# A decoder step on one core: the first half-step in the form of the second (one microbatch alone, two by seven products for eight), its down sums in PSUM, and the state-space matrices made in larger batches

## The chip, the cores and the metric

The kernel runs on one core of one Trainium2 chip, with one launch. The metric is device time in microseconds (us) of that core; the time before is the median of three runs. All data are fp32. TensorE (PE) multiplies, VectorE (DVE), ScalarE (ACT) and GpSimd (POOL) work on tiles, and DMA transfers are issued from two queues here: SyncE's (SP), which loads, and ACT's, which mostly stores. Each engine takes its instructions in the order of its own queue.

## The reference

One decoder layer, run on a prompt of 1024 tokens and 8 x 4 sample tokens that share the weights. With D = 1024 and D_FF = 2816 = 22 x 128:

```python
def swiglu(x, w_gate, w_up, w_down):
    return (silu(x @ w_gate) * (x @ w_up)) @ w_down

h = h + 0.5 * rms_norm(swiglu(rms_norm(h, g_pre), w_gate1, w_up1, w_down1), g_post)   # first half-step
z = rms_norm(h, g_mix) @ w_in                 # -> u (state-space input), q, k, v
# u: 32 groups of a complex diagonal state-space scan (state 64, width 16), gelu, gate
# q, k, v: sliding-window attention (window 128), rotary, sinks
h = h + rms_norm(concat(norm(y_ssm), norm(o)) @ w_out, g)
h = h + rms_norm(memory_attend(rms_norm(h, g), mem_k, mem_v), g)
h = h + 0.5 * rms_norm(swiglu(rms_norm(h, g_pre), w_gate2, w_up2, w_down2), g_post)   # second half-step
```

The change touches the two half-steps and the making of the state-space matrices (`s5_discretise` and the powers of the discretised state, which depend on weights alone).

## The kernel before

**Tokens and precision.** The 1056 tokens are three microbatches t = 0, 1, 2 of NT = 352 columns; t = 2 holds the last prompt tokens and the samples. Activations lie transposed, 8 chunks of 128 features by 352 tokens. A product of fp32 matrices is made of three matmuls (`PASSES`): weight and activation are each split into a rounded high part (an ACT copy) and the rest (a DVE subtraction). `loadw` does so for a weight: one transfer of 512 KB into one of two `raw` buffers, ACT (L99), DVE (L100), into one of six `w` tiles. One row block of weight (1024 wide) feeds 24 matmuls of 128x128 by 128x352 for each microbatch.

**First half-step (`ffn`, L393).** For each g of 11 (two of the 22 hidden blocks), gate and up are computed for all three microbatches with the same split weights (`gate_up`, L223: matmuls of L105), the hidden tiles `hid` stay in SBUF, and `down` (L235, matmuls of L241) follows for each microbatch; the part sums of each g leave PSUM through a DVE addition into an SBUF sum (L247). In the gaps between, `filler()` draws one step of `ssm_prep`, a generator: tables by powers of two for four groups at a time (`tables`), then matrices of one group at a time (`groups`), stored in DRAM scratch `sp`; the matrix M goes through a padded DRAM tile `kp`, written and read back on ACT's queue (L723, L725). `finish1` does the post-norm, the residual and the next pre-norm.

**Second half-step.** Microbatch 0 goes alone through `ffn_one` (L252), gate, up and down interleaved as above. Microbatches 1 and 2 then form a 2x2 block product with seven products for eight: `pair_operands` (L273) makes sums and differences of the two and splits them (L280) into `xq` slots of 4 x 352; `pair_weights` (L298) does the same for two weight row blocks, 512 wide; `pair_products` (L326) multiplies, matmuls of L330; `pair_gate_up` writes the hidden to DRAM `hs`. `pair_down` (L373, matmuls of L385) reads it back for each hidden block k, splits it, and sums all 22 blocks in PSUM. PSUM has eight banks, of which six (`bank`) and two (`pbank`) can be had. The first of the two downs uses all eight at once (parts `((0, 8),)`), the second goes through the blocks twice with four banks each (parts `((0, 4), (4, 4))`), so that each 512-wide piece of weight feeds 12 matmuls.

**Order.** The program is written with a priority for each piece and put into each engine's queue by a planner that simulates the engines. The order of a queue is then fixed; a wait in it holds up all behind it on that engine.

Of the kernel before, what the change touches and what calls it, by code (L numbers as in the profile page):

```python
# [6 lines left out]
F32 = mybir.dt.float32  # L7
# [15 lines left out]
PASSES = ((0, 0), (0, 1), (1, 0))  # L23
G_FFN1_PRE, G_FFN1_POST, G_MIX_PRE, G_MIX_POST, G_XA_PRE, G_XA_POST, G_FFN2_PRE, G_FFN2_POST, G_MEM, G_CAT = range(10)
# [3 lines left out]
def decoder_step(tc, a, o):  # L28
# [194 lines left out]
    def gate_up(x, w, h, j):  # L223
        pg, pu = bank(), bank()
        for p, ww in ((pg, w[0]), (pu, w[1])):
            for k in range(8):
                mm3(p[:, :NT], ww, k * 128, x, k, k == 0, k == 7)
        s, u = R("sg", [128, NT], 2), Q()
        v.tensor_mul(s, pg[:, :NT], x[2])  # L229
        sc.activation(s, s, AF.Silu)  # L230
        v.tensor_mul(u, pu[:, :NT], x[2])  # L231
        v.tensor_mul(s, s, u)  # L232
        split(s, h[:, j, 0], h[:, j, 1])

    def down(acc, w, h, first):  # L235
        for cs in (range(4), range(4, 8)):
            p = {c: bank() for c in cs}
            for j in range(2):
                for c in cs:
                    for i, (wa, xa) in enumerate(PASSES):  # L240
                        pe.matmul(p[c][:, :NT], w[j][:, wa, c * 128:c * 128 + 128], h[:, j, xa],  # L241
                                  start=j == 0 and i == 0, stop=j == 1 and i == 2)
            for c in cs:
                if first:
                    sc.activation(acc[:, c], p[c][:, :NT], AF.Copy)
                else:
                    v.tensor_add(acc[:, c], acc[:, c], p[c][:, :NT])  # L247

    def hidden(bufs):
        return R("hid", [128, 2, 2, NT], bufs, F32R)  # L250

    def ffn_one(x, wg, wu, wd, home):  # L252
        acc, held = None, None
        for g in range(NH // 2 + 1):
            now = None
            if g < NH // 2:
                ws = [(loadw(wg[2 * g + j]), loadw(wu[2 * g + j])) for j in range(2)]
                now = hidden(2)
                for j in range(2):
                    gate_up(x, ws[j], now, j)  # L260
            if held is not None:
                ds = [loadw(wd[2 * (g - 1) + j]) for j in range(2)]
                acc = K8(home) if acc is None else acc
                down(acc, ds, held, g == 1)
            held = now
        return acc
# [3 lines left out]
    def slot(dtype=F32R):  # L270
        return xp[0].tile([128, 4, NT], dtype, name="xq", tag="xq", bufs=12)

    def pair_operands(ya, yb, home):  # L273
# [8 lines left out]

        t3 = slot(F32)
# [69 lines left out]
    def pair_gate_up(x, wg, wu, hs, home):  # L353
# [7 lines left out]
        for j in range(NH // 2):  # L361
# [11 lines left out]
    def pair_down(wd, hs, i, y, parts):  # L373
        for c0, n in parts:
            p = [bank() if c < 6 else pbank() for c in range(n)]
            for k in range(NH):
                h, x = slot(), R("raw2", [128, 1024], 2)[:, :NT]
                hi, lo = h[:, 0], h[:, 1]
                sy.dma_start(x, hs[k][:, i])
                sc.activation(hi, x, AF.Copy)  # L380
                v.tensor_sub(lo, x, hi.bitcast(F32))
                w = loadw(wd[k][:, c0 * 128:(c0 + n) * 128], width=n * 128)
                for c in range(n):
                    for q, (wa, xa) in enumerate(PASSES):
                        pe.matmul(p[c][:, :NT], w[:, wa, c * 128:c * 128 + 128], (hi, lo)[xa],  # L385
                                  start=k == 0 and q == 0, stop=k == NH - 1 and q == 2)
            for c in range(n):
                if c % 2:
                    v.tensor_copy(y[:, c0 + c], p[c][:, :NT])
                else:  # L390
                    sc.activation(y[:, c0 + c], p[c][:, :NT], AF.Copy)

    def ffn(xn, wg, wu, wd, order, home, finish, filler, ready=None):  # L393
        acc = {}

        for g in range(NH // 2):
            if g == 0 and ready:
                ws, ds = ready
            else:
                ws = [(loadw(wg[2 * g + j]), loadw(wu[2 * g + j])) for j in range(2)]  # L400
                ds = [loadw(wd[2 * g + j]) for j in range(2)]
            hid = {}

            def gu(t):
                hid[t] = hidden(3)
                for j in range(2):
                    gate_up(xn[t], ws[j], hid[t], j)
                    filler()

            last = g == NH // 2 - 1  # L410
            for n in (0, 1, 3, 4, 2, 5) if last else (0, 1, 3, 2, 4, 5):
                what, t = "down" if n > 2 else "gu", order[n % 3]
                if what == "gu":
                    gu(t)
                else:
                    if g == 0:
                        acc[t] = K8(home[t])
                    down(acc[t], ds, hid[t], g == 0)
                    if last:
                        finish(t, acc[t])  # L420
                    else:
                        filler()
# [30 lines left out]
    rd = scratch("rd", [128, 256])  # L453
    hd = [[scratch(f"h{i}_{t}", [128, 8, NT]) for t in range(3)] for i in range(3)]
# [48 lines left out]
    def ssm_prep():  # L503
# [21 lines left out]
        par = take(97)  # L525
        ar, ai, ls, s1 = par[:, 0:32], par[:, 32:64], par[:, 64:96], par[:, 96:97]
# [118 lines left out]

        def tables(q):
            pos[0] = base
            C = take(512).rearrange("p (g c) -> p g c", c=128)
            Z = take(512).rearrange("p (g c) -> p g c", c=128)
            u = take(256).rearrange("p (g c) -> p g c", c=64)  # L650
            w = take(256).rearrange("p (g c) -> p g c", c=64)
            v.memset(C[:, :, 0], 1.0)
            v.memset(Z[:, :, 0], 0.0)
            for k in range(7):
                m = 1 << k
                bc = TBC[:, k, 4 * q:4 * q + 4][:, :, None].to_broadcast([128, 4, m])
                bs = TBS[:, k, 4 * q:4 * q + 4][:, :, None].to_broadcast([128, 4, m])
                tt(u[:, :, :m], C[:, :, :m], bc)
                tt(w[:, :, :m], Z[:, :, :m], bs)
                tt(C[:, :, m:2 * m], u[:, :, :m], w[:, :, :m], ALU.subtract)  # L660
                tt(u[:, :, :m], C[:, :, :m], bs)
                tt(w[:, :, :m], Z[:, :, :m], bc)
                tt(Z[:, :, m:2 * m], u[:, :, :m], w[:, :, :m], ALU.add)
            for i in range(4):
                sc.dma_start(spd[4 * q + i][:, SP_COS:SP_COS + 128], C[:, i])
                sc.dma_start(spd[4 * q + i][:, SP_SIN:SP_SIN + 128], Z[:, i])

        def groups(q):
# [17 lines left out]
            wt, out = take(128), take(528)  # L686
            w8, cx = out[:, 0:256], out[:, 256:528]
            clx, cls = cx[:, 0:144], cx[:, 144:272]
            t1, t2 = take(144), take(144)

            def j3(x, n=9):
                return x.rearrange("p (j h) -> p j h", h=16)[:, :n]

            for i in range(4):
                g = 4 * q + i

                def hb(x, n):
                    return x[:, i][:, None, :].to_broadcast([128, n, 16])

                def jb(x, j0, n):  # L700
                    return x[:, g, j0:j0 + n][:, :, None].to_broadcast([128, n, 16])

                tt(j3(t1), hb(C1, 9), jb(LR, 0, 9))
                tt(j3(t2), hb(C2, 9), jb(LI, 0, 9))
# [25 lines left out]
        for _ in range(11):  # L730
            yield
# [795 lines left out]
```

## Time and profile before

| what | value |
|---|---|
| median of 3 runs | 2355.25 us (2351.96 to 2357.52) |
| profiled execution | 2350.7 us, span 2348.9 us |
| granted TensorE clock, mean | 0.986 |
| first half-step and first projection | 0 to about 895 us of the span |
| state-space, attention, memory parts | about 895 to 1596 us |
| second half-step | about 1596 us to the end |
| moved by DMA | 272 MB, mean 116 GB/s |

The profile is of one execution; a term worked out from it stands against 2350.7 us, which is 4.55 us under the median. In rows of stretches the columns are: from:to, length, busy time of each engine with its number of instructions, granted clock, share of DMA time, GB/s. In rows of groups they are: line, engine, operation, output and input with their shapes, count, busy us, mean ns of one, and the idle time of the engine just before them with what ended it. In a timeline they are start, duration, engine and line; SPq and ACTq are the issuing of transfers from these queues.

### The profile page before, as it was taken

The page shows a single profiled execution, that of the slowest core. Times are in us where ns is not written, and L with a number is a line of the kernel's source. Part 1 is how long each engine was busy: PE and PEld are TensorE (multiplying, and loading weights), DVE is VectorE, ACT ScalarE, POOL GpSimd, SP SyncE. Part 2 cuts the span into 40 slices and gives each one's busy share as a digit, 9 for nine tenths or more (in the row PEclk, how much of TensorE's full clock was granted, in tenths as well). Part 3 has the DMA queues.
Part 4 walks back from the last instruction along what each step waited for, and adds up shares of the span by engine and source line. Part 5 has one row for each costly group of instructions (what it writes and reads, how often), then busy time and mean ns, then how long its engine had stood idle before and what let it go on. Part 6 is the DMA issues. An engine that isn't in the chain of part 4 may idle for free.

```text
span 2348.9 us, 37434 instructions
## 1 busy us (share of the span) xinstructions
PE 2281.9 (97%) x14425; PEld 2178.3 (93%) x14425; DVE 1631.5 (69%) x4004; ACT 839.4 (36%) x1645; POOL 15.9 (1%) x54
## 2 busy tenths in 40 slices
PE   8999999999999899999799989999999899999997
PEld 8999999999999899888699869999999899999996
DVE  8756556665664877777768855588866987776464
ACT  6322111211212433535545323354433434344443
POOL 0000000000000000000000000000000000000000
PEclk9999999999999999999899999999999999999998
DMA  4222212221213321544135562165544243326663
GB/s 171 70 71 68 62 57 71 82 76 59 73 55 93 112 87 58 193 147 127 35 97 167 183 221 72 55 213 169 175 132 144 85 143 106 115 97 200 185 193 119
DMA packets 112194, 272.39 MB, mean 116 GB/s; under 512 B 13168, under 2 KB 54128, under 8 KB 110576
## 3 DMA queue, kind: packets, MB, share of 16 engines
q1 hardware_dynamic: 78976, 227.81, 30.8%
q10 hardware_dynamic: 33040, 42.20, 5.1%
q8 instruction: 113, 1.85, 0.3%
q14 instruction: 65, 0.53, 0.1%
HBM read 229.87 MB, written 43.20 MB: 116 GB/s over the span
## 4 chain that ended last, share of the span: by engine, by line
PE 85%; DVE 7%; DMA 5%; ACT 2%; issue 1%; ACTq 0%; SPq 0%; DVEq 0%
PE mm L105 39%; PE mm L241 14%; PE mm L330 13%; PE mm L385 3%; PE px L105 3%; DMA raw<-wd 2%; DVE w L100 1%; PE cv L1279 1%; PE cs L1254 1%; PE px L1176 1%; DVE K L219 1%; PE ac L877 1%; PE px L495 1%; PE px L385 1%; DMA K<-h 1%
## 5 line engine op out<-in xcount | busy, mean ns | idle before, releaser
L105 PE MATMUL mm<-X,w 128*128 128x352 f32 x6384 | 1060.8, 325 | 12.3 <-ACT X L195 6.5
L105 PEld LDWEIGHTS mm<-X,w 128*128 128x128 f32 x6384 | 1028.3, 189 | 30.2 <-ACT X L195 8.5
L99 ACT ACTIVATE w<-raw 128x1024 fp32r<-128x1024 f32 (+1 forms) x271 | 266.2, 988 | 500.4 <-PE mm L105 212.2
L100 DVE TENSOR_TENSOR w<-raw,w 128x1024 fp32r<-128x1024 f32 (+1 forms) x271 | 307.1, 1136 | 136.2 <-ACT w L99 134.0
L241 PE MATMUL mm<-hid,w 128*128 128x352 f32 x2112 | 358.6, 328 | 12.6 <-DVE K L247 6.2
L241 PEld LDWEIGHTS mm<-hid,w 128*128 128x128 f32 x2112 | 345.6, 189 | 19.7 <-DVE K L247 8.8
L330 PE MATMUL mm<-xq,w 128*128 128x352 f32 x1584 | 263.5, 323 | 0.0
L330 PEld LDWEIGHTS mm<-xq,w 128*128 128x128 f32 x1584 | 255.9, 188 | 0.4 <-ACT w L310 0.4
L247 DVE TENSOR_TENSOR K<-K,mm 128x352 f32<-128x352 f32 x320 | 158.3, 518 | 52.2 <-PE mm L241 51.3
L514 DVE TENSOR_TENSOR K<-K 128x128 f32<-128x128 f32 (+7 forms) x796 | 171.6, 250 | 11.3 <-DMA sp<-K 2.0
L385 PE MATMUL mm<-xq,w 128*128 128x352 f32 x924 | 159.1, 326 | 4.6 <-ACT w L99 3.4
L385 PEld LDWEIGHTS mm<-xq,w 128*128 128x128 f32 x924 | 148.8, 188 | 10.7 <-ACT w L99 5.9
L310 ACT ACTIVATE w<-raw 128x512 fp32r<-128x512 f32 x154 | 90.0, 625 | 119.1 <-PE mm L330 83.1
L231 DVE TENSOR_TENSOR q<-mm,rs 128x352 f32<-128x352 f32 x88 | 46.0, 522 | 117.6 <-PE mm L105 117.6
L311 DVE TENSOR_TENSOR w<-raw,w 128x512 fp32r<-128x512 f32 x154 | 101.1, 686 | 6.2 <-ACT w L310 3.9
L116 DVE TENSOR_TENSOR tot<-tot,sq 128x352 f32<-128x352 f32 x179 | 93.0, 520 | 10.4 <-ACT sq L114 7.0
L114 ACT ACTIVATE sq<-K 128x352 f32<-128x352 f32 x170 | 81.9, 490 | 42.7 <-DVE tot L116 34.7
L229 DVE TENSOR_TENSOR sg<-mm,rs 128x352 f32<-128x352 f32 x88 | 46.0, 523 | 72.9 <-PE mm L105 72.5
L183 ACT ACTIVATE hid<-sg 128x352 fp32r<-128x352 f32 x88 | 43.6, 496 | 145.7 <-DVE sg L232 115.7
L230 ACT ACTIVATE sg<-sg 128x352 f32<-128x352 f32 x88 | 43.2, 492 | 138.9 <-DVE sg L229 120.4
L195 ACT ACTIVATE X<-K,c_gains 128x352 fp32r<-128x352 f32 x80 | 44.0, 580 | 45.4 <-DVE K L220 42.8
L184 DVE TENSOR_TENSOR hid<-sg,hid 128x352 fp32r<-128x352 f32 x88 | 45.8, 521 | 15.6 <-ACT hid L183 15.4
(326 smaller groups left out, 2179.1 us busy)
## 6 DMA issues: line engine op xcount, KB each, us to landing
raw<-wd SPq DMA_DIRECT2D x66, 512.0 KB
raw<-wu SPq DMA_DIRECT2D x65, 512.0 KB
raw<-wg SPq DMA_DIRECT2D x64, 512.0 KB
sp<-sp SPq DMA_DIRECT2D x16, 848.0 KB
h<-K ACTq DMA_DIRECT2D x9, 1408.0 KB
raw<-hs SPq DMA_DIRECT2D x66, 176.0 KB
raw<-wd SPq DMA_DIRECT2D x44, 256.0 KB
K<-xT SPq DMA_DIRECT2D x24, 352.0 KB
```

The costliest lines, as they stand in the source:

```text
L99: sc.activation(w[:, 0], raw, AF.Copy)
L100: v.tensor_sub(w[:, 1], raw, w[:, 0].bitcast(F32))
L105: pe.matmul(p, w[:, wa, col:col + 128], x[xa][:, k, :n], start=first and i == 0, stop=last and i == 2)
L114: sc.activation(q, c, AF.Square)
L116: eng.tensor_add(tot, tot, q)
L241: pe.matmul(p[c][:, :NT], w[j][:, wa, c * 128:c * 128 + 128], h[:, j, xa], start=j == 0 and i == 0, stop=j == 1 and i == 2)
L247: v.tensor_add(acc[:, c], acc[:, c], p[c][:, :NT])
L310: sc.activation(w[:, 0], x, AF.Copy)
L311: v.tensor_sub(w[:, 1], x, w[:, 0].bitcast(F32))
L330: pe.matmul(p, w[a_][:, wa, k * 128:k * 128 + 128], x[b_][xa][:, k], start=start and k == 0 and i == 0, stop=stop and k == 3 and i == 2, s ...
L385: pe.matmul(p[c][:, :NT], w[:, wa, c * 128:c * 128 + 128], (hi, lo)[xa], start=k == 0 and q == 0, stop=k == NH - 1 and q == 2)
L514: v.tensor_tensor(out, x, y, op)
```

## The change

Both half-steps get the same form. In the first, microbatch `ta` = 2 goes alone through gate and up for all 22 blocks, then its down; then `tb` = 0 and `tc_` = 1 go through gate and up as a pair by seven products, then their two downs. In the second, microbatch 0 alone also does all its gate and up first, then its down. The hidden goes to DRAM (`h1`, `h2`) and is read back for the down, in pairs of blocks (`hidden(2)`, two buffers) instead of `xq` slots; all down sums stay in PSUM over the 22 blocks. The parts are `((0, 8),)` for a microbatch alone, where the scale `rs` is applied as the sum is moved out, and `((0, 4), (4, 4))` for both of the pair in the first half-step. `xq` has 8 slots instead of 12. Between the pieces, `step` draws the preparation by a table: `F_A = (0, 0, 1, 1)` steps per piece.

```diff
+F_A = (0, 0, 1, 1)
-    def gate_up(x, w, h, j):
+    def gate_up(x, w, out):
...
-        v.tensor_mul(u, pu[:, :NT], x[2])
-        v.tensor_mul(s, s, u)
-        split(s, h[:, j, 0], h[:, j, 1])
+        v.tensor_mul(s, s, pu[:, :NT])
+        sc.dma_start(out, s)
-    def down(acc, w, h, first):
-        for cs in (range(4), range(4, 8)):
...
-                    v.tensor_add(acc[:, c], acc[:, c], p[c][:, :NT])
+    def down(wd, h, y, parts, rs=None, filler=lambda: None):
+        for c0, n in parts:
+            p = [bank() if c < 6 else pbank() for c in range(n)]
+            for k in range(NH):
+                if k % 2 == 0:
+                    pair = hidden(2)
+                x = R("raw2", [128, 1024], 2)[:, :NT]
+                hi, lo = pair[:, k % 2, 0], pair[:, k % 2, 1]
+                sy.dma_start(x, h[k])
+                sc.activation(hi, x, AF.Copy)
+                v.tensor_sub(lo, x, hi.bitcast(F32))
+                w = loadw(wd[k][:, c0 * 128:(c0 + n) * 128], width=n * 128)
+                for c in range(n):
+                    for q, (wa, xa) in enumerate(PASSES):
+                        pe.matmul(p[c][:, :NT], w[:, wa, c * 128:c * 128 + 128], (hi, lo)[xa],
+                                  start=k == 0 and q == 0, stop=k == NH - 1 and q == 2)
+                filler()
...
+    for j in range(NH):
+        ws = pre[2 * j:2 * j + 2] if j < 2 else (loadw(a["wg1"][j]), loadw(a["wu1"][j]))
+        gate_up(xa, ws, h1[j][:, 2])
+        if 5 <= j and j % 2:
+            step()
+        if j == 3:
+            for t in (tb, tc_):
+                xr[t] = load_x(t, a["xT"][t])
+                norm_in_place(xr[t], G_FFN1_PRE)
+    y = K8(ta)
+    down(a["wd1"], [h[:, 2] for h in h1], y, ((0, 8),), xa[2], lambda: step(F_A[1]))
+    ops = pair_operands(xr[tb], xr[tc_], tc_, ta)
+    post1(ta, y)
+    pair_gate_up(ops, a["wg1"], a["wu1"], [h[:, 0:2] for h in h1], tb, lambda: step(F_A[2]))
...
+    pre1(ta, y)
+    for i, t in enumerate((tb, tc_)):
+        y = K8((tc_, tb)[i])
+        down(a["wd1"], [h[:, i] for h in h1], y, ((0, 4), (4, 4)), filler=lambda: step(F_A[3]))
+        if i:
+            for _ in prep:
+                pass
+        marks[t] = tc.cur_priority
+        post1(t, y, load_x((ta, 3)[i], a["xT"][t]))
+        pre1(t, y)
...
+    for j in range(NH):
+        gate_up(xn[0], (loadw(a["wg2"][j]), loadw(a["wu2"][j])), h2[j][:, 2])
+    y = K8(3)
+    down(a["wd2"], [h[:, 2] for h in h2], y, ((0, 8),), xn[0][2])
```

In the preparation, one doubling works on cosine and sine together (`double`), the first 16 columns for all 32 groups at once, the rest for four groups; two groups at a time are made into matrices, with one transposition and one small product each, and M goes through a zeroed scratch `kd`:

```diff
+        def double(T, tmp, k, gs, n):
+            m = 1 << k
+            bc, bs = (t[:, k, gs][:, None, :, None].to_broadcast([128, 2, n, m]) for t in (TBC, TBS))
+            u = tmp[:, :2 * n * m].rearrange("p (z g m) -> p z g m", z=2, m=m)
+            tt(T[:, :, :, m:2 * m], T[:, :, :, :m], bc)
+            tt(u, T[:, :, :, :m], bs)
+            tt(T[:, 0, :, m:2 * m], T[:, 0, :, m:2 * m], u[:, 1], ALU.subtract)
+            tt(T[:, 1, :, m:2 * m], T[:, 1, :, m:2 * m], u[:, 0], ALU.add)
...
-            for i in range(4):
+            for i in (0, 2):
...
+                for n in range(2):
+                    pe.transpose(p3[:, n], wt[:, n], ident)
...
-                sc.dma_start(kd, kp[:16])
...
+                sc.dma_start(kd[g:g + 2, :, 128:256].rearrange("g h c -> h g c"),
+                             kp[:16].rearrange("h (g c) -> h g c", g=2))
```

Where it moves instructions, in the queues of the two programs. First PE in the first half-step, about the first weight blocks of before: a gate and up of one microbatch (L105), a down of two hidden blocks (96 matmuls of L241), the next gate and up.

```order
203 L105 MATMUL mm<-X_290,w 128x352
204 L105 MATMUL mm<-X_289,w 128x352 x2
205 L105 MATMUL mm<-X_290,w 128x352
206 L105 MATMUL mm<-X_289,w 128x352
207 L241 MATMUL mm<-hid,w 128x352 x96
208 L105 MATMUL mm<-X_134,w 128x352
209 L105 MATMUL mm<-X_135,w 128x352
```

After, at the end of the 22 gates and ups of microbatch 2 (L106), its whole down begins (L252); `mm` are six of its banks, `px` two.

```order
711 L106 MATMUL mm<-X_166,w 128x352
712 L106 MATMUL mm<-X_165,w 128x352
713 L252 MATMUL mm<-hid,w 128x352 x15
714 L252 MATMUL px<-hid,w 128x352 x6
715 L252 MATMUL mm<-hid,w 128x352 x21
716 L252 MATMUL px<-hid,w 128x352 x6
```

The downs, which lay between the gates and ups, have moved behind all of them, as 528 matmuls in a row.

Second, ACT in the first half-step, where it makes the matrices of one group before: weight splits (L99), the copies of the transposed product (L715, L716), of M (L721), a hidden split (L183), and the stores, with the write and the reading back of `kp` (L723, L725).

```order
360 L99 ACTIVATE w<-raw 128x1024
361 L715 ACTIVATE K_411<-px 128x128
362 L716 ACTIVATE K_411<-px 128x64
363 L721 ACTIVATE kp<-px 16x128
364 L183 ACTIVATE hid<-sg 128x352
365 L726 DMA sp_114<-K_411 128x192
366 L723 DMA kp_5883<-kp 16x256
367 L727 DMA sp_114<-K_411 128x272
368 L725 DMA sp_114<-kp_5883 128x1x128
369 L99 ACTIVATE w<-raw 128x1024 x2
```

After, in the first half-width down (`tb`, parts `((0, 4), (4, 4))`): hidden splits (L247) and 512-wide weight splits (L100), with the work of one pair of groups between.

```order
528 L247 ACTIVATE hid<-raw_6523 128x352
529 L100 ACTIVATE w<-raw 128x512 x2
530 L694 DMA sp_116<-K_707 256x1x192
531 L700 DMA kd<-kp 16x2x128
532 L684 DMA sp_117<-K_707 256x1x144
533 L705 DMA sp_116<-kd 128x1x128 x2
534 L682 ACTIVATE K_707<-K_707 64x2x128
535 L685 DMA sp_117<-K_707 128x1x128
536 L686 DMA sp_117<-K_707 128x1x128
537 L692 ACTIVATE K_707<-px 128x2x128
538 L693 ACTIVATE K_707<-px 128x2x64
539 L699 ACTIVATE kp<-px 16x256
```

A group's work has moved from between gates and ups of three microbatches into a loop of narrow weight splits, two groups at a time.

Third, DVE in the second half-step, where microbatch 0 ends and the pair begins. Before, the operands' sums (L284, L285) and splits (L280) lie among the last additions of the down (L247), the last gate's product and the pair's first weights (L311 and following).

```order
2434 L285 TENSOR_TENSOR K_15541<-K_15541,K_15148 128x1408
2435 L247 TENSOR_TENSOR K_16191<-K_16191,mm 128x352 x2
2436 L317 TENSOR_TENSOR raw<-raw 128x512
2437 L247 TENSOR_TENSOR K_16191<-K_16191,mm 128x352
2438 L280 TENSOR_TENSOR xq<-xq 128x1408
2439 L247 TENSOR_TENSOR K_16191<-K_16191,mm 128x352
2440 L184 TENSOR_TENSOR hid<-sg,hid 128x352
2441 L247 TENSOR_TENSOR K_16191<-K_16191,mm 128x352
2442 L280 TENSOR_TENSOR xq<-K_15148,xq 128x1408
```

After, they come right behind the last gate and up of microbatch 0 (L235), ahead of the down's third pair of hidden blocks (L248).

```order
2431 L235 TENSOR_TENSOR sg<-sg,mm 128x352
2432 L282 TENSOR_TENSOR xq<-K_15552 128x1408
2433 L101 TENSOR_TENSOR w<-raw,w 128x1024
2434 L283 TENSOR_TENSOR K_15552<-K_15552,K_15159 128x1408
2435 L275 TENSOR_TENSOR X_18210<-K_15159,X_18210 128x1408
2436 L275 TENSOR_TENSOR xq<-xq 128x1408
2437 L275 TENSOR_TENSOR xq<-K_15159,xq 128x1408
2438 L101 TENSOR_TENSOR w<-raw,w 128x1024
2439 L275 TENSOR_TENSOR xq<-K_15552,xq 128x1408
2440 L248 TENSOR_TENSOR hid<-raw_17492,hid 128x352
2441 L248 TENSOR_TENSOR hid<-raw_17525,hid 128x352
```

The operands have moved from the end of the down to its beginning. In all, the built programs have 13522 and 13248 matmuls on PE (the first half-step's gates, ups and downs 4752 and 4488), 3991 and 3608 instructions on DVE, 550 and 826 transfers in SP's queue, 257 and 284 in ACT's, 44 and 12 fills on POOL.

More of the change, by code (lines that the diff above doesn't have):

```diff
@@ L220, in postnorm, with hidden @@
             v.tensor_add(y[:, k], resid(k), y[:, k])
-    def gate_up(x, w, h, j):
+    def hidden(bufs):
+        return R("hid", [128, 2, 2, NT], bufs, F32R)
+    def gate_up(x, w, out):
         pg, pu = bank(), bank()
@@ L227, in gate_up @@
                 mm3(p[:, :NT], ww, k * 128, x, k, k == 0, k == 7)
-        s, u = R("sg", [128, NT], 2), Q()
+        s = R("sg", [128, NT], 2)
         v.tensor_mul(s, pg[:, :NT], x[2])
         sc.activation(s, s, AF.Silu)
-        v.tensor_mul(u, pu[:, :NT], x[2])
-        v.tensor_mul(s, s, u)
-        split(s, h[:, j, 0], h[:, j, 1])
-    def down(acc, w, h, first):
-        for cs in (range(4), range(4, 8)):
[L237 to L245, printed above, removed]
-                else:
-                    v.tensor_add(acc[:, c], acc[:, c], p[c][:, :NT])
@@ L249, in hidden @@
[L249 to L266, printed above, removed]
+        v.tensor_mul(s, s, pu[:, :NT])
@@ L281, in halves_of, with both @@
             ops[name] = (hi, lo)
+        def both(x):
+            return x[:, 0:4], x[:, 4:8]
         t3 = slot(F32)
@@ L371, in pair_gate_up @@
                 sc.dma_start(hs[2 * j + i], h[:, 2 * i:2 * i + 2])
[L373 to L422, printed above, removed]
+            filler()
@@ L425, in decoder_step, with norm_in_place, by_chunk, get @@
+    def norm_in_place(y, gi):
+        rs = rstd_wide(sqsum([y[:, k] for k in range(8)]))
+        for k in range(8):
+            v.scalar_tensor_tensor(y[:, k], y[:, k], gain(gi, k), rs, op0=ALU.mult, op1=ALU.mult)
+    def by_chunk(src):
+        def get(k):
+            x = total()
+            sy.dma_start(x, src[:, k])
+            return x
+        return get
     gains = cload(const, "gains", [128, 88])
@@ L649, in tables @@
[L649 to L663, printed above, removed]
+            T = take(1024).rearrange("p (z g c) -> p z g c", z=2, c=128)
@@ L685, in groups, with j4 @@
             tt(bb2, bb2, t64, ALU.add)
[L686 to L692, printed above, removed]
-            for i in range(4):
+            clx, t2, wt, w8 = (take(n).rearrange("p (g c) -> p g c", g=2) for n in (288, 288, 256, 384))
+            def j4(x, n):
+                return x.rearrange("p g (j h) -> p g j h", h=16)[:, :, :n]
@@ L1359, in after_o @@
             return
-        rs = rstd_wide(sqsum([y[:, k] for k in range(8)]), tag="rs", bufs=3)
-        for k in range(8):
-            v.scalar_tensor_tensor(y[:, k], y[:, k], gain(G_FFN2_PRE, k), rs, op0=ALU.mult, op1=ALU.mult)
+        norm_in_place(y, G_FFN2_PRE)
         xn[t] = y
```

161 lines of the change are left out of this document (89 added, 72 removed).

## The prediction

> **What bounds the kernel now.** I read the page first.
>
> ```profile
> span 2348.9 us, 37434 instructions
> PE 2281.9 (97%) x14425; PEld 2178.3 (93%) x14425; DVE 1631.5 (69%) x4004; ACT 839.4 (36%) x1645; POOL 15.9 (1%) x54
> PE 85%; DVE 7%; DMA 5%; ACT 2%; issue 1%; ACTq 0%; SPq 0%; DVEq 0%
> ```
>
> TensorE is busy for 97% and carries 85% of the chain that ended last, so only two things move the time: fewer matmuls, or fewer microseconds in which PE does less than it could. The next view is busy time in stretches (columns: stretch; its length, then PE, PEld, DVE, ACT, POOL busy and instructions; granted clock; DMA share; GB/s). 0 to 895.2 is the first half-step with the state-space preparation beside it and, at its end, the first projection; 1596 to 1870 is the second half-step's microbatch alone, 1880 to 2140 its pair by seven products, then two down stages.
>
> ```profile
> 0.00:50.00 50.00, 41.60 (x234) 39.83 (x235) 43.05 (x149) 34.58 (x67) 0.59 (x6) 0.97 0.55 200
> 50.00:750.00 700.00, 699.91 (x4328) 685.93 (x4327) 449.56 (x1375) 146.08 (x298) 5.84 (x30) 1.00 0.23 68
> 750.00:895.20 145.20, 136.80 (x830) 134.08 (x829) 100.28 (x249) 48.72 (x94) 1.96 (x2) 0.94 0.27 92
> 1820.00:1880.00 60.00, 52.57 (x309) 50.33 (x308) 56.54 (x95) 29.22 (x45) 0.00 (x0) 0.97 0.26 84
> 1880.00:2140.00 260.00, 260.00 (x1625) 260.00 (x1624) 200.56 (x342) 104.95 (x178) 0.00 (x0) 1.00 0.36 117
> 2140.00:2226.00 86.00, 86.00 (x536) 86.00 (x534) 43.03 (x57) 34.03 (x52) 0.00 (x0) 1.00 0.68 213
> 2270.00:2320.00 50.00, 45.98 (x263) 41.46 (x262) 24.61 (x43) 22.23 (x44) 0.00 (x0) 1.00 0.59 181
> ```
>
> The same view for single lines gives the yardstick: what one 128x352 matmul costs where nothing waits (L330, the seven products), and how many of them each stretch of the first half-step held (L105 gate, up and projection; L241 down), with the prep's own matmuls (L714, L720).
>
> ```profile
> 1900.00:2142.00 242.00, 242.00 (x1512) 242.00 (x1510) 1.00 0.35 115
> ...
> 0.00:50.00 50.00, 37.25 (x192) 34.37 (x192) 0.97 0.55 200
> 50.00:750.00 700.00, 453.75 (x2796) 447.60 (x2797) 1.00 0.23 68
> 750.00:895.20 145.20, 104.91 (x614) 100.08 (x613) 0.94 0.27 92
> ...
> 0.00:50.00 50.00, 1.88 (x12) 2.04 (x13) 0.97 0.55 200
> 50.00:750.00 700.00, 238.98 (x1430) 231.22 (x1428) 1.00 0.23 68
> 750.00:895.20 145.20, 27.53 (x144) 26.11 (x144) 0.94 0.27 92
> ...
> 50.00:750.00 700.00, 8.67 (x32) 4.55 (x32) 1.00 0.23 68
> ...
> 50.00:750.00 700.00, 12.56 (x64) 3.56 (x64) 1.00 0.23 68
> ```
>
> 242.00/1512 is 0.160 us per matmul. By it the first 50 us hold 204 x 0.160 = 33 us of work (17 lost), the next 700 hold 4226 x 0.160 = 676 (24 lost), the last 145.2 hold 758 x 0.160 = 121 (24 lost). The page's busy share hides this, because neighbouring matmuls overlap in it.
>
> **The change, part by part, against the profiled run (2350.7 us, 4.6 under the median of 2355.25).**
>
> *Seven products for eight in the first half-step.* Gate and up of two microbatches go from 2112 matmuls to 1848: 264 x 0.160 = **-42.2 us**. This is on the path, since PE bounds that stretch, and the built program has the 264 fewer.
>
> *Start.* What PE waits for in the first half-step:
>
> ```profile
> PE mm L105 <- ACT X L195: 6.5, 1, 6.5
> PE mm L241 <- ACT hid L183: 3.1, 1, 3.1
> PE mm L241 <- DVE hid L184: 2.8, 1, 2.8
> ```
>
> The 6.5 us until the first X is ready stay. Of the other 11 of the 17 lost I take **-4** (0 to -8): only one microbatch is prepared at first, the other two load at the fourth weight pair under PE work.
>
> *Down sums stay in PSUM.* Vanishing adds:
>
> ```profile
> L247 DVE TENSOR_TENSOR K<-K,mm 128x352 f32<-128x352 f32 x320 | 158.3, 518 | 52.2 <-PE mm L241 51.3
> ```
>
> They free DVE, which is no bound (450 of 700 us). For PE only the gaps at gate/down borders count: of the 24 us lost in 50 to 750, the prep's matmuls take between half of their busy 21.2 (busy spans overlap; a 0.160 matmul shows 0.325) and all of it. I take 15 for them, which stay, and **-9** (-3 to -13).
>
> *End of the first half-step.* Today all three microbatches finish together in the last 145 us: the waits of 3.1 and 2.8 above, and a clock of 0.94 (0.06 x 145 = 8.7 us). Now two are normed under later downs, and one is left at the end: 24 lost becomes about 9, **-15** (0 to -20).
>
> *Half-width downs, the price of the change.* With two accumulating downs in 4+4 banks, every 512-wide piece of weight carries 12 matmuls, 12 x 0.160 = 1.92 us. The kernel already does this once, in its last down (L385; its window, its weight splits on ACT, PE's and ACT's waits there):
>
> ```profile
> 2231.20:2328.00 96.80, 91.32 (x529) 84.14 (x527) 1.00 0.57 175
> ...
> L99 ACT ACTIVATE w<-raw x26: 629/632/637, 2267.5 to 2324.6; 128x512 fp32r<-128x512 f32 x26
> ...
> PE mm L385 <- ACT w L99: 3.4, 6, 1.6
> ...
> ACT w L99 <- DMA raw<-wd: 33.6, 23, 2.9
> ```
>
> 529 matmuls take 96.8 us where 84.6 would do; weights come one per (2324.6-2267.5)/25 = 2.28 us. The timeline shows why: two raw buffers, each reloaded only after both splits.
>
> ```profile
> 2266.01 0.33 SPq L92 DMA_DIRECT2D raw<-wd  x1
> ...
> 2269.31 0.63 ACT L99 ACTIVATE w<-raw 128x512 fp32r<-128x512 f32 x1 [0.81 <-DMA raw<-wd]
> ...
> 2269.97 0.69 DVE L100 TENSOR_TENSOR w<-raw,w 128x512 fp32r<-128x512 f32 x1 [0.70 <-ACT w L99]
> ...
> 2270.70 0.33 SPq L92 DMA_DIRECT2D raw<-wd  x1
> ```
>
> Issue to landing 3.3, ACT 0.63, DVE 0.69: 4.69 us for one buffer, two pieces per cycle, 2.35 each. The first half-step gets 2 downs x 2 halves x 22 = 88 such pieces: between 88 x 0.28 (12.2/44, the down as a whole) = 25 and 88 x (2.35 - 1.92) = 38. The hidden tiles come on the same SP queue there too, so the row fits. I take 26, less 6 for the six split weights PE has ahead at the start of the first: **+20** (0 if the loop keeps up, 38). SP's queue, 550 transfers before and 826 after, is no bound: four issues of 0.33 to 0.37 in a cycle of 4.69. The full-width down of one microbatch is free: 86.00 of 86.00 busy in 2140 to 2226.
>
> A rule of the Trainium skill speaks against this stage: "TensorE: Matmul & The Clock Gate", section "HAM oscillation", says that a loop over K with compute per tile shorter than its wait for data lets the clock drop to half at every tile, once the idle time passes about 3.4 us. The row of 2270 to 2320 shows 1.00 in just this loop, with waits of 0.6 us on average, so the sum goes by the row; by the rule it would be rival four.
>
> *Preparation in larger batches.* Prep's tensor operations leave DVE about 380 instructions shorter, off the path (POOL's memsets, 44 to 12, too: 15.9 us busy in all). What is on the path is where it now lies. Nothing but its tables runs in the first down, 22 steps run in the pair, and 7 group pairs in the first half-width down, where ACT feeds PE: four activations and seven DMA issues each on ACT's queue, two of them waiting for a write to return. Rows of before for the pieces:
>
> ```profile
> 224.36 0.39 ACTq L723 DMA_DIRECT2D kp<-kp  x1
> ...
> 225.88 0.66 ACTq L725 DMA_DIRECT2D sp<-kp  x1
> ...
> ACT w L99 <- DMA sp<-K: 14.2, 1, 14.2
> ```
>
> From that write's issue to the read's are 1.5 us; with five more issues of 0.33 to 0.39 and the activations (some 0.3 each) I estimate 4.7 us of ACT per pair of groups, beside a loop that already lacks time; part lies in ACT's idle share (50 - 22 of 50). I take **+10** for the seven (0 to 20). The 14.2 us row shows how long a weight split can stand behind a store.
>
> *Pair under prep.* DVE is 200.56/260 = 77% busy in the second half-step's pair, without a loss. Here prep's groups come on top:
>
> ```profile
> L514 DVE TENSOR_TENSOR K<-K 128x128 f32<-128x128 f32 (+7 forms) x796 | 171.6, 250 | 11.3 <-DMA sp<-K 2.0
> ```
>
> Halved in number, the group part is by estimate 57 of these (a third, at larger tiles); two thirds of it in the pair make 37 us, so 91%. Since DVE works in order, a late split then stalls PE: **+6** (0 to 15). Norms that stand ahead of weight splits in DVE's queue during half-width downs: 24 operations of 0.5 us for each microbatch, **+5** (0 to 10). First half-step: -42.2-4-9-15+20+10+6+5 = -29.
>
> *Second half-step.* The 303 matmuls between 1820 and 1880 need 48.5 us; 11.5 are lost where the operands are made after the last gate:
>
> ```profile
> PE mm L241 <- DVE K L247: 5.0, 5, 2.0
> PE mm L330 <- ACT w L310: 2.4, 1, 2.4
> L280 DVE TENSOR_TENSOR xq<-K,xq 128x1408 fp32r<-128x1408 f32 x5 | 8.0, 1615 | 0.0
> ```
>
> Now a whole down (528 x 0.160 = 84 us) lies between, under which the operands are made. In DVE's order seven operations of that size or nearly (L282, L283, four L275, with two weight splits of 1.2) come before the third hidden pair: about 12.5 us, which PE needs 15.5 us after the start of the down (four pieces x 24 x 0.160). Five weights are ready (19 us). **-11.5** and **+1** (0 to 5). The last two downs take the hidden in pairs, four pieces ahead instead of a dozen slots: **+2** (0 to 4). Together -8.5.
>
> Sum: -29.2 - 8.5 = **-37.7**: 2313 for the profiled run, 2355.25 - 37.7 = 2317.6 for the median. I say **2318**.
>
> **The rivals.**
>
> *One: as summed, -15 to -60.* For it: the matmuls are counted, and the half-width price is read in the same kind of loop.
>
> *Two: cheaper loops, 2272 to 2295.* The first half-step's half-width downs have no output stores beside them; if a load lands in 2.5 us instead of 3.3, a buffer cycles in 3.9 and a piece in 1.95: the +20 and the +10 are gone, and with the pair stage free too (-6) the sum is -74, 2281. Against it: DMA share is 0.59 in that stage and stores of the prep join.
>
> *Three: slower, by ACT's queue.* If the group pairs don't take 1.4 us each (10/7) but more, everything else as summed, the gain is gone at (10 + 37.7)/7 = 6.8 us each, and it is slower by more than 0.2% at 7.5 us. The 14.2 us wait behind one sp store is above that; against it, such a wait occurs once in 845 us. At 10 us each: 2378. If they cost between, the result is within the noise.
>
> *Four: the clock.* At half clock a half-width piece costs 3.84 us: 88 x 1.92 = +169, about 2470. Against it the 1.00.
>
> **How the numbers follow.** A difference under 0.2% (4.7 us) can't be told from none here. Chances: one 0.58, two 0.17, a gain of 5 to 15 us 0.09, within 5 us 0.07, three 0.07, four 0.02. Faster is 0.84, same 0.07, slower 0.09. The range: the low end takes half of case two (2286); the high end goes to a gain of 7 us (2348), because half-width at 38, prep at 20, pair at 15 and norms at 10 (+42 together) leave about none. Outside lie some 0.08 below and 0.13 above.
>
> **What would show it.** L330's successor 1848 matmuls twice, at 0.160 in the first pair; weight splits 512 wide in the first half-step every 2.2 to 2.35 us with ACT waiting for raw, PE short by 25 us over its four halves; waits of PE behind ACT in the first of them, none in the second; no gap at 1820. The prediction is wrong if 512-wide pieces come at 1.95 us or less, if the first half-width down lasts 20 us longer than the second, or if the clock there falls under 0.95.

## The result, and the profile after

The changed kernel takes 2337.91 us (median of 4, 2334.64 to 2339.88) against 2355.11 before: ratio 0.9926, 95% interval 0.9909 to 0.9944, a gain of 17 us where 37 were forecast, inside the stated range. In the profiled execution (2338.15 us) the page begins:

```profile
span 2336.4 us, 37554 instructions
PE 2241.9 (96%) x14141; PEld 2133.5 (91%) x14141; DVE 1667.1 (71%) x3621; ACT 991.9 (42%) x1872; POOL 8.6 (0%) x22
...
PE 53%; DMA 11%; DVE 6%; ACT 3%; issue 1%; ACTq 0%; SPq 0%; DVEq 0%
```

PE is busy for 40 us less, but the span is only 12.5 shorter: PE now waits more. (The shares of the chain that ended last can't be set beside those of before: it can be followed back only to 603 us, and they add up to 74%. In what there is of it DMA has 11 of 74, where it had 5 of 100.) To see where, cut both traces at the same event, the first matmul of the state-space input (the same instruction order follows it in both for some 700 us). Stretches before and after that cut, first of the kernel before, then of the changed one:

```profile
0.00:895.20 895.20, 878.32 (x5388) 859.84 (x5389) 592.88 (x1771) 229.38 (x458) 8.39 (x38) 0.99 0.25 79
895.20:2348.90 1453.70, 1403.63 (x9039) 1318.45 (x9037) 1038.60 (x2234) 610.06 (x1187) 7.47 (x16) 0.98 0.43 138
```

```profile
0.00:894.70 894.70, 844.84 (x5104) 818.34 (x5105) 668.11 (x1482) 384.38 (x693) 2.15 (x6) 0.99 0.53 168
894.70:2336.40 1441.70, 1397.06 (x9039) 1315.16 (x9037) 998.98 (x2140) 607.47 (x1179) 6.46 (x16) 0.99 0.45 145
```

All of the gain, 12.0 us, comes behind the cut, about 10.5 of it in the second half-step itself. The first half-step has 284 matmuls fewer in the trace and takes as long as before. Its stages in the changed kernel, by the lines of PE: gates and ups of one microbatch to 182.5, its down to 268, the pair from 272.8 to 588, and then the two half-width downs, which I cut near each 264th matmul of L252 into four quarters (one microbatch, four of eight row blocks). The stages, the last row of which is the second half-step where microbatch 0 ends and the pair begins, then the quarters:

```profile
0.00:182.50 182.50, 174.57 (x1072) 172.52 (x1073) 152.92 (x411) 84.65 (x116) 0.20 (x4) 1.00 0.65 206
182.50:272.80 90.30, 86.25 (x531) 85.67 (x530) 67.09 (x129) 35.25 (x54) 0.00 (x0) 0.99 0.71 210
...
819.30:894.70 75.40, 74.32 (x466) 73.14 (x466) 38.49 (x90) 17.04 (x30) 0.00 (x0) 1.00 0.20 67
...
1800.00:1860.00 60.00, 60.00 (x375) 60.00 (x374) 38.13 (x75) 24.41 (x43) 0.00 (x0) 1.00 0.37 120
```

```profile
581.95:658.50 76.55, 59.99 (x334) 54.67 (x334) 46.39 (x115) 33.36 (x77) 0.00 (x0) 0.93 0.67 211
658.50:709.50 51.00, 45.84 (x265) 42.03 (x264) 27.74 (x50) 26.29 (x52) 0.00 (x0) 1.00 0.67 194
709.50:768.20 58.70, 49.14 (x280) 46.53 (x280) 44.26 (x100) 33.25 (x68) 1.95 (x2) 0.94 0.65 206
768.20:819.30 51.10, 46.81 (x272) 42.85 (x271) 28.86 (x52) 26.70 (x51) 0.00 (x0) 1.00 0.64 197
```

A quarter is 264 x 0.160 = 42.2 us of matmul. The four take 237.4; without 24 matmuls of the pair that lie in the first (3.8 us), 64.6 us are lost in them (the small matmuls of preparation and norms take part of this). Two are quiet (51), the first holds the preparation and the end of microbatch 2's norm (76.6), the third microbatch 0's norms (58.7). The cuts lie 3 to 10 matmuls early; cut exactly, the quarters are 77.9, 50.5, 61.1 and 50.4, so the quarters in this text are good to some 2 us, where nothing else is said. No engine is near full in them: DVE 62%, ACT 50%, DMA 66%. What PE waits for in all four, and what ACT waits for in a quiet one:

```profile
PE mm L252 <- ACT hid L247: 21.9, 25, 2.2
PE mm L252 <- DVE hid L248: 10.5, 5, 3.0
```

```profile
ACT w L100 <- DMA raw<-wd: 21.9, 20, 2.0
ACT hid L247 <- DMA raw<-h: 2.4, 3, 1.3
```

PE waits for split hidden tiles, ACT waits for weights: this is a queue in which hidden splits stand behind weight splits that wait for their transfer. In the quiet second quarter the chain that ended last goes round the weights alone, load, ACT's split, DVE's split, next load:

```profile
660.10 3.07 DMA raw<-wd
...
663.20 0.64 ACT w L100
...
663.86 0.70 DVE w L101
664.58 3.02 DMA raw<-wd
```

Ten such turns, from 660.10 to 705.40, take 4.5 us each, for two pieces.

### The profile page after: what moved, and what is told of

Same layout as the page of the kernel before. It is cut to its first block, busy times and chain, and to the rows that moved or that the text cites. A ratio compares the mean times of both kernels' runs of the same rounds, so it can differ in the third digit from the quotient of the medians.

```text
span 2336.4 us, 37554 instructions
## 1 busy us (share of the span) xinstructions
PE 2241.9 (96%) x14141; PEld 2133.5 (91%) x14141; DVE 1667.1 (71%) x3621; ACT 991.9 (42%) x1872; POOL 8.6 (0%) x22
## 4 chain that ended last, share of the span: by engine, by line
PE 53%; DMA 11%; DVE 6%; ACT 3%; issue 1%; ACTq 0%; SPq 0%; DVEq 0%
PE mm L106 17%; PE mm L327 13%; PE mm L252 6%; DMA raw<-wd 5%; PE px L106 3%; DVE w L101 2%; PE px L252 2%; DMA raw<-h 2%; ACT w L100 1%; PE cs L1253 1%; PE cv L1278 1%; PE ac L876 1%; PE px L457 1%; PE px L1175 1%; DVE K L220 1%
## 5 line engine op out<-in xcount | busy, mean ns | idle before, releaser
L106 PE MATMUL mm<-X,w 128*128 128x352 f32 x4272 | 709.3, 326 | 10.8 <-ACT X L196 7.1
L106 PEld LDWEIGHTS mm<-X,w 128*128 128x128 f32 x4272 | 685.8, 188 | 25.5 <-ACT X L196 7.3
L252 PE MATMUL mm<-hid,w 128*128 128x352 f32 x2772 | 486.7, 331 | 39.9 <-ACT hid L247 25.7
L252 PEld LDWEIGHTS mm<-hid,w 128*128 128x128 f32 x2772 | 456.0, 191 | 58.4 <-ACT hid L247 36.9
L100 ACT ACTIVATE w<-raw 128x1024 fp32r<-128x1024 f32 (+1 forms) x359 | 322.4, 900 | 412.4 <-DMA raw<-wd 129.3
L327 PE MATMUL mm<-xq,w 128*128 128x352 f32 x2112 | 359.8, 324 | 4.0 <-DVE K L257 4.0
L327 PEld LDWEIGHTS mm<-xq,w 128*128 128x128 f32 x2112 | 342.4, 189 | 6.0 <-DVE K L257 4.3
L307 ACT ACTIVATE w<-raw 128x512 fp32r<-128x512 f32 x308 | 178.4, 624 | 206.2 <-PE mm L327 119.8
L308 DVE TENSOR_TENSOR w<-raw,w 128x512 fp32r<-128x512 f32 x308 | 202.2, 687 | 15.8 <-ACT w L307 11.8
L327 PE MATMUL mm<-X,w 128*128 128x352 f32 x1056 | 185.7, 324 | 1.2 <-DVE sq L342 0.7
L327 PEld LDWEIGHTS mm<-X,w 128*128 128x128 f32 x1056 | 171.0, 188 | 3.3 <-DVE sq L342 1.0
L248 DVE TENSOR_TENSOR hid<-raw,hid 128x352 fp32r<-128x352 f32 x198 | 97.9, 521 | 64.5 <-ACT hid L247 60.1
L247 ACT ACTIVATE hid<-raw 128x352 fp32r<-128x352 f32 x198 | 90.6, 490 | 98.4 <-DMA raw<-h 50.9
L476 DVE TENSOR_TENSOR K<-K 128x256 f32<-128x256 f32 (+4 forms) x380 | 106.9, 320 | 26.2 <-DMA sp<-K 9.2
L327 PE MATMUL mm<-K,w 128*128 128x352 f32 x528 | 99.7, 326 | 0.0
L327 PEld LDWEIGHTS mm<-K,w 128*128 128x128 f32 x528 | 88.3, 190 | 0.3 <-ACT w L307 0.3
L252 PE MATMUL px<-hid,w 128*128 128x352 f32 x396 | 75.4, 324 | 0.0
L252 PEld LDWEIGHTS px<-hid,w 128*128 128x128 f32 x396 | 66.2, 188 | 0.0
```

Source lines behind the costliest of these rows:

```text
L100: sc.activation(w[:, 0], raw, AF.Copy)
L106: pe.matmul(p, w[:, wa, col:col + 128], x[xa][:, k, :n], start=first and i == 0, stop=last and i == 2)
L307: sc.activation(w[:, 0], x, AF.Copy)
L308: v.tensor_sub(w[:, 1], x, w[:, 0].bitcast(F32))
L327: pe.matmul(p, w[a_][:, wa, k * 128:k * 128 + 128], x[b_][xa][:, k], start=start and k == 0 and i == 0, stop=stop and k == 3 and i == 2, s ...
L476: v.tensor_tensor(out, x, y, op)
```

## The experiments

Ratios are to the kernel before on the same chip; "quarters" are the four of the half-width downs, in us, cut as above.

| run | edit | ratio (95% interval) | quarters |
|---|---|---|---|
| changed | | 0.9926 (0.9909 to 0.9944) | 76.5, 51.0, 58.7, 51.1 |
| e1 | prep in the pair | 0.9905 (0.9889 to 0.9922) | 58.0, 51.0, 57.9, 50.1 |
| e2 | weights of two blocks per load | 1.0001 (0.9990 to 1.0013) | 76.7, 57.1, 60.9, 49.1 |
| e3 | e1 and e2 | 0.9918 (0.9894 to 0.9942) | 61.6, 47.1, 58.2, 54.7 |
| e7 | hidden of two blocks per buffer | 0.9948 (0.9931 to 0.9965) | 66.0, 53.9, 58.3, 49.3 |
| e8 | e2 and e7 | 0.9822 (0.9803 to 0.9840) | 66.0, 49.2, 46.8, 45.0 |
| e9 | e8 and prep in the pair | 0.9757 (0.9738 to 0.9777) | 56.2, 42.5, 46.5, 45.0 |
| e10 | e9, norms written later | 0.9763 (0.9747 to 0.9779) | 55.0, 42.5, 46.7, 45.4 |
| e12 | e1, full-width downs | 0.9852 (0.9835 to 0.9868) | 52.5, 42.6, 65.5, 42.5 |
| e13 | e12 and e7 | 0.9837 (0.9822 to 0.9852) | 54.4, 42.6, 65.1, 42.5 |

**The second half-step alone (e5).** The kernel before, with only the second half-step in the changed form.

> The first half-step and the preparation as before, the second half-step in the changed form (microbatch 0 whole, its down after all gates, hidden in pairs). Theory (the end of the span after the first projection carries all of the gain, 12 of 12.5 us by the two traces): 2341 to 2347 against 2355 before, the junction before the pair without its 11.5 us. Rival (the first half-step gives part of the gain): 2349 to 2355.

2340.35 against 2351.27, ratio 0.9953 (0.9935 to 0.9970): 7 to 15 us. The second half-step gives 11 us by itself, most of the changed kernel's 17. By the cut the first half-step's part is 0.5 us; by these medians it is up to 6, but the two intervals overlap.

**The preparation out of the half-width down (e1).**

```diff
-F_A = (0, 0, 1, 1)
+F_A = (0, 0, 2, 0)
```

> F_A = (0, 0, 2, 0): the preparation that ran in the first half-width down of the first half-step runs in the pair instead. Theory (ACT's queue: work on pairs of groups stands between the weight splits there and waits for DMA round trips, 4 us a pair): the first half-width quarter, 78 us in the changed kernel from 582 to 660, falls to about 52 like the second; the pair gets 4 to 10 us longer; in all 2318 to 2326 against 2338. Rival (the loop of two raw buffers alone makes the loss, the preparation fits into its waits): the quarter stays over 70 us, in all 2335 to 2345.

The first quarter falls by 18.5 us, but the pair's end moves from 582 to 592, so that some 9 us remain: the preparation did lengthen that quarter, but the total (2330.67 against 2351.27 before) is only 5 us under the changed kernel by ratio, less than expected, and the intervals overlap. Not all of the 18.5 is ACT's queue: 36 of the preparation's own matmuls, 6 us of PE busy, moved along. In the changed kernel's timeline ACT is seen standing in that quarter:

```profile
604.49 0.69 ACTq L700 DMA_DIRECT2D kd<-kp  x1
604.58 0.61 ACT L100 ACTIVATE w<-raw 128x512 fp32r<-128x512 f32 x1
...
607.25 1.40 ACTq L705 DMA_DIRECT2D sp<-kd  x2
...
609.40 0.42 ACT L682 ACTIVATE K<-K 64x256 f32<-64x256 f32 x1 [4.21 <-DMA sp<-kd]
...
610.67 0.88 ACT L247 ACTIVATE hid<-raw 128x352 fp32r<-128x352 f32 x2 [0.85 <-ACT K L682]
...
611.22 8.28 PE L252 MATMUL mm<-hid,w 128*128 128x352 f32 x40 [2.22 <-ACT hid L247]
```

From 605.19 to 609.40 ACT computes nothing: the reading back of `kd` in its queue is issued at 607.25, 2.8 us after the write, and takes 1.40 to issue; another store follows, then the prep's copy, and only then the hidden tiles that PE has waited 2.22 us for. The waits of ACT that the profile puts down to stores in the whole first quarter:

```profile
ACT rs L158 <- DMA sp<-K: 7.1, 1, 7.1
...
ACT K L682 <- DMA sp<-kd: 4.2, 1, 4.2
ACT hid L247 <- DMA sp<-kd: 3.4, 1, 3.4
```

The third is the plainest, a hidden split that stands behind the reading back of `kd`. The first isn't shown to be a store's doing: `rs` is the scale of microbatch 2's norm, and it started at 601.54, as PE's product for it (L144) ended at 601.51.

**Wider weight loads (e2), and both (e3).**

```diff
+                elif k % 2 == 0:
+                    raw = wp.tile([128, 1024], F32, name="raw", tag="raw", bufs=2)
+                    sy.dma_start(raw.rearrange("p (k c) -> p k c", k=2),
+                                 wd[k:k + 2, :, c0 * 128:c0 * 128 + 512].rearrange("k p c -> p k c"))
+                    w, o_ = loadw(None, raw), 0
```

> Half-width downs load the weights of two hidden blocks in one transfer of 512 KB, split at width 1024; all else as in the changed kernel, the same bytes. Theory (two raw buffers, each a 256 KB load of about 3 us and two splits, give a piece only every 2.2 to 2.4 us where PE needs 1.92): the undisturbed quarters fall from 52 and 49 us to about 44, the last down of the second half-step from 97 to about 88; in all 2305 to 2318. Rival one (the hidden pair's two buffers bind, or DMA throughput): no change, 2333 to 2343. Rival two (the loop is latency bound but the other quarters are lost to ACT's queue): only the three quiet stages gain, 20 us, 2316 to 2320.

> Both edits, the preparation in the pair and two hidden blocks per load. If the two losses are separate they add: 2285 to 2300. If the wider loads already hide the preparation (PE then has a reserve of weights), it is no faster than the wider loads alone.

e2 is a miss: 57.1 and 49.1 in the quarters that had 51, the last down of the second half-step at 101 us (97 in the changed kernel), and in all some 18 us over the changed kernel. Part of this is the clock, 0.87, 0.94 and 0.92 in its first three quarters. e3 (2332.71) is as fast as the preparation moved alone, 19 us under e2: the wider loads add nothing to that in the total, though its second quarter is at 47.1, and neither of the two cases expected for it came. By e2's waits the weights are seldom late now. ACT's waits in its second quarter:

```profile
ACT w L100 <- PE mm L260: 17.4, 10, 3.5
ACT hid L247 <- DMA raw<-h: 11.3, 12, 1.4
```

and a turn of it:

```profile
701.99 1.05 SPq L246 DMA_DIRECT2D raw<-h  x2
...
703.70 1.06 ACT L100 ACTIVATE w<-raw 128x1024 fp32r<-128x1024 f32 x1 [1.57 <-PE mm L260]
...
705.55 0.50 ACT L247 ACTIVATE hid<-raw 128x352 fp32r<-128x352 f32 x1 [0.79 <-DMA raw<-h]
...
706.09 4.15 PE L260 MATMUL mm<-hid,w 128*128 128x352 f32 x24 [0.49 <-ACT hid L247]
...
706.63 2.17 SPq L246 DMA_DIRECT2D raw<-h  x2
```

ACT now mostly waits for PE to give a `w` tile back, so weights are ahead; but the two `raw2` buffers of the hidden turn in 706.63 - 701.99 = 4.64 us for two blocks, as the weights did (the prediction's 4.69). There are two rings (buffers that are loaded, split and loaded again in turn), of the same length. That is a new theory, from one turn: each ring gives two blocks in about 4.6 us, PE needs 3.84.

**The hidden ring alone (e7), and both rings (e8).**

```diff
-                x = R("raw2", [128, 1024], 2)[:, :NT]
...
+                    x = R("raw2", [128, 1024], 2)[:, :2 * NT].rearrange("p (k n) -> p k n", k=2)
+                    for m in range(2):
+                        sy.dma_start(x[:, m], h[k + m])
+                    sc.activation(pair[:, :, 0], x, AF.Copy)
+                    v.tensor_sub(pair[:, :, 1], x, pair[:, :, 0].bitcast(F32))
```

> All downs: the hidden tiles of two blocks go by two transfers into one raw2 buffer and are split by one ACT copy and one DVE subtraction, so four blocks are in flight where two were; the weights as in the changed kernel. Theory now (two rings of two buffers run beside each other in a half-width down, weights and hidden, each about 4.6 us for two blocks, so that widening one alone leaves the other): quiet quarters stay at 49 to 52 us, total within 5 us of the changed kernel (ratio to before 0.990 to 0.995). Rival (the hidden ring alone binds, the weights do not): quarters of 45 to 46, ratio 0.980 to 0.985.

> Hidden pairs per load as in the run before, and weights of two blocks per transfer. Theory (both rings): the quiet quarters fall to 43 to 46 us each (264 x 0.160 = 42.2), the last down of the second half-step to 86 to 90; preparation still disturbs the first quarter (65 to 76); ratio to before 0.978 to 0.986. Rival (what is left is DMA throughput or the order of ACT's queue): quarters stay at 49 or more, ratio 0.990 to 1.000.

e7 alone leaves the quiet quarters at 54 (4.3 of it one wait at the border to the first; 49.7 if cut exactly) and 49, and its ACT waits in the second nearly for weights alone:

```profile
ACT w L100 <- DMA raw<-wd: 29.4, 21, 3.9
```

Together they gain: 2310.19 against 2354.20, the third and fourth quarter at 46.8 and 45.0, the last down of the second half-step at 92 us instead of 97. Neither ring alone gains in the total, both together do: so both bound the loop. The wide form has more blocks in flight and also fewer instructions on ACT and DVE; no run adds buffers alone, so the two aren't told apart. What doesn't fit: the last down at 92 is above the 86 to 90 expected, and the second quarter stays at 49.2. In that quarter the trace has the last pair of groups of the preparation, one wait of PE of 3.1 us right behind it, and a clock of 0.97; with the preparation moved (e9) it is 42.5.

**Both rings and the preparation (e9), norms later (e10).**

> Both rings wide, and the preparation out of the half-width down, in the pair. Theory: all four quarters under 52 us, first quarter about 50, the pair 10 us longer as it was when only the preparation was moved; ratio to before 0.972 to 0.980. Rival (with wide rings the preparation is hidden where it was): no faster than wide rings alone.

> As the run before, and microbatch 0's post-norm and next pre-norm written behind the first quarter of microbatch 1's down, so that they have lower priority than its loads. Theory (the third quarter's 8 us over the others are norms ahead of splits in DVE's and ACT's queues): third quarter 45 to 50, total 5 to 10 us under the run before. Rival (the norms are only moved into the last quarter or to the projection): no difference of more than 3 us.

e9 takes 2294.69 against 2354.20. Its quarters:

```profile
594.90:651.10 56.20, 51.80 (x300) 51.43 (x300) 37.51 (x55) 28.78 (x42) 0.00 (x0) 0.91 0.74 233
651.10:693.60 42.50, 42.50 (x264) 42.50 (x263) 25.35 (x27) 21.30 (x28) 0.00 (x0) 1.00 0.76 228
693.60:740.10 46.50, 44.79 (x276) 43.63 (x275) 39.90 (x68) 27.30 (x43) 1.95 (x2) 1.00 0.73 235
740.10:785.10 45.00, 45.00 (x284) 45.00 (x283) 26.55 (x37) 22.51 (x30) 0.00 (x0) 1.00 0.70 223
```

```profile
ACT hid L247 <- PE mm L261: 20.5, 10, 2.2
```

In the second quarter, 264 matmuls in 42.50 us, PE is the bound, and ACT waits for PE, as the last line says. The DMA share is higher than in the changed kernel (0.76 against 0.67), so throughput was no limit there. The rings' reserve also takes up the norms of the third quarter, 46.5 for 58.7; the first, 56.2 with 3.8 of the pair in it, misses the expected 50, with one wait of PE of 4.2 us at the border to the pair and a clock of 0.91. The reserve doesn't take up the preparation: from e8 to e9, where it only moves, are 15 us. e10 makes no difference, as its rival forecast; the 8 us over the others that it was to win back in the third quarter had shrunk to 4 in e9.

**Full width (e12, e13).** The price by its root: with 24 matmuls for each piece the rings have 24 x 0.160 = 3.84 us a block.

```diff
-        down(a["wd1"], [h[:, i] for h in h1], y, ((0, 4), (4, 4)), ...
+        down(a["wd1"], [h[:, i] for h in h1], y, ((0, 8),), ...
```

> The changed kernel with the preparation in the pair and both downs of the first half-step's pair full width ((0, 8), all eight PSUM banks, 24 matmuls for each piece of weight); rings as in the changed kernel, and microbatch 0's norm has no free bank until its down has ended. Theory (the price lies in the half width, with 12 matmuls, 1.92 us, for each turn of rings that need 2.3): the two downs take 2 x 88 us = 176 in place of 217 with the preparation moved, less what the norm's wait for a bank costs between the downs and at the end (5 to 15): ratio to before 0.974 to 0.982. Rival (the stage loses to stores, norms and the clock, whatever the width): downs over 200 us, ratio 0.986 to 0.992.

> As the run before, with the hidden of two blocks split at once from one raw2 buffer. Theory: a full-width piece gives both rings 3.87 us a block, so a wider hidden ring buys nothing: within 3 us of the run before. Rival (ACT's and DVE's fixed cost for each instruction or the hidden ring matters there as well): 5 us or more faster.

e12 takes 2315.93 against 2350.93. With the old rings its second and fourth quarter (here the halves of a down by blocks) take 42.6 and 42.5; between the downs a norm, which needs a bank, leaves PE with one gap, at a clock of 0.84 in that stretch:

```profile
644.70:687.30 42.60, 42.60 (x265) 42.60 (x264) 20.21 (x24) 17.95 (x27) 0.00 (x0) 1.00 0.62 195
687.30:752.80 65.50, 48.94 (x288) 48.05 (x288) 39.84 (x83) 27.55 (x49) 1.94 (x2) 0.84 0.44 142
752.80:795.30 42.50, 42.50 (x264) 42.50 (x263) 18.72 (x21) 16.16 (x24) 0.00 (x0) 1.00 0.58 182
```

```profile
PE px L152 <- DVE tot L117: 15.9, 1, 15.9
```

So the quiet quarters' loss comes from the half width, and the kernel buys something with it: no such gap. The ratio is above the 0.974 to 0.982 expected and the two downs take 203 us (3.8 of the pair in it), where 176 and 5 to 15 more were expected and the rival had over 200: the gap takes 16 us, and the clock comes on top. e13's gain of 0.15% lies within the intervals.

**Again, on one chip (e14, e15).** The changed kernel and e9:

> The changed kernel itself on the same chip as the next: ratio to before 0.991 to 0.995, as first measured.

> Both rings wide and the preparation in the pair, beside the changed kernel on one chip: ratio to before 0.974 to 0.978, 35 to 45 us under the changed kernel.

2339.88 (0.9943, 0.9921 to 0.9964) and 2297.50 (0.9770, 0.9752 to 0.9788), before 2351.28. e9's form beats both kernels, by 42 us the changed one.

## Why the prediction was wrong

- *Seven products, -42.2; start, -4:* right. L327 ran its 1848 matmuls, 295.7 us by 0.160, between 272.8 and 588; the first stage lost 182.5 - 1056 x 0.160 = 13.5 us, forecast 13.
- *Down borders, -9; pair under prep, +6:* the 315 us of the pair hold 17 us beyond its own matmuls and 14 of the down's, and 4 stand in front of it, where 15 for prep's matmuls plus 6 were forecast. The sum is right, in part by luck: the 4 us are a wait for the operands, DVE is 85% busy instead of 91%, and 36 of prep's 96 matmuls lie in the first quarter and not here.
- *End of the first half-step, -15:* the last 75.4 us hold 432 projection matmuls (69); 6 lost where 9 were left in the sum.
- *Half-width downs, +20:* this is the first failed step. The quiet quarters take 51.0 and 51.1, 8.85 over 42.2, which makes 35 for four. The row I read it from was right (2.32 us a block here, 2.28 there). Wrong were a price of 0.295 us a block (26/88) between the ends of 0.28 and 0.43, where 0.40 was measured, and the 6 us taken off for a reserve, of which no run shows anything. That there are two rings was not seen. The down of the kernel before loads its hidden into two buffers as well, and its timeline had the turn: loads issued at 2266.45 and, two loads on, at 2271.13, 4.7 us for two blocks. The waits hid it, with 33.6 us of ACT's put down to weights and 1.7 to the hidden.
- *Prep in the half-width down, +10 (0 to 20):* second failed step. The first quarter is 76.5 - 3.8 - 51.0 = 21.7 above a quiet one; moving the preparation out takes 18.5 of it. The estimate had 4.7 us of ACT for each pair of groups, 33 for seven, and let 23 of them vanish in ACT's idle share. With six pairs in the trace 21.7 did not vanish (36 matmuls of prep and the end of microbatch 2's norm are in it). It also took 1.5 us from the write's issue to the read's, which took 1.9 to 4.8 for these six pairs; a hidden split that PE needs stood behind such a read for 3.4 us.
- *Norms, +5:* 58.7 - 51 = 7.7 in the third quarter (10.6 if cut exactly), within the 0 to 10 or just over.
- *Second half-step, -8.5:* 12.0 by the cut (about 10.5 without what lies ahead of it), 11 by e5. The gap before the pair is gone (no PE wait from 1790 to 1880).

The three terms of the quarters were +35 together and measured 64.6; the missing 30 us are the forecast's error. They were priced one by one, as if each could hide in idle time of ACT, in a loop where PE already waited. That the loop's slowness is what made the disturbances dear isn't shown: moving the preparation away gained 15 us with wide rings (e8 to e9), and by ratio 5 with narrow ones (e1).

Rival two (the loop costs nothing) needed a cycle of 3.9 us and got 4.6. Rival three named the right place, ACT's queue behind stores, but at about 3.6 us for each of six group pairs it doesn't decide alone. Rival four happened in part: the clock is 0.93 and 0.94 in the disturbed quarters, at most 76.55 x 0.07 + 58.7 x 0.06 = 9 us of the 64.6 (PE also waits while it is low), and 1.00 in the quiet ones. The Trainium skill's rule ("TensorE: Matmul & The Clock Gate", "HAM oscillation") names idle gaps of more than about 3.4 us. This trace differs: the clock fell, though the longest single wait of PE in the quarters is 3.0 us. I had read the 1.00 of a quiet loop as if it held for a disturbed one. Of the signs named beforehand this one came, a clock under 0.95 in two quarters (0.96 over the whole first down); the first down was 18 us longer than the second, not 20.

## What to carry to other kernels

Count every ring of buffers that feeds a loop, its turn (issue to landing, then each split) over its depth in blocks, and compare all of them with what PE needs for a block; here widening one of two equal rings gained nothing, and widening both took 24 us (by ratio) off the changed kernel. Price other work in the same queues with its waits, not at its busy time alone; a reserve of loaded blocks took up the norms here, but not the preparation. Halving the width of a piece halves the time that each turn has: check it before trading a full-width down for free banks.

## What the runs showed of the hardware

From the issue of a load to the split that waited for it were 3.3 us for 256 KB (2266.01 to 2269.31, kernel before) and 3.6 us for the first of two loads of 176 KB (701.99 to 705.55, e2). From the issue of the small write of `kd` to the issue of its reading back were 1.9 to 4.8 us.

A wait of PE of 2 us was enough for the granted clock to fall. In the first half-step of the changed kernel it fell to half six times. In the 3.4 us before each fall PE stood for 2.0 to 2.5 us; in the other stretches of this length, laid end to end with these from 12 us on, it stood for 1.5 us at most. One fall, the stretch before it and its own:

```profile
609.02:612.43 3.41, 1.21 (x7) 1.21 (x8) 0.71 (x2) 2.18 (x5) 0.00 (x0) 1.00 0.55 168
612.43:615.84 3.41, 3.41 (x14) 3.41 (x13) 3.38 (x8) 1.47 (x6) 0.00 (x0) 0.50 0.64 185
```

The other traces draw the line less sharply: in the kernel before the clock fell once after 1.5 us idle, and in e12 once it did not after 1.9.
